# Ordering a two-block transformer's instructions with the compiler's other timing model

## The chip, the cores and the metric

The kernel runs on one NeuronCore of one Trainium2 chip. The metric is the device time of one execution in microseconds (us), lower is better. The core has five engines that run side by side, each through its own queue in order: PE (TensorE, matmul, with its weight loads shown as PEld), DVE (VectorE), ACT (ScalarE), POOL (GpSimd) and SP (SyncE, here only issuing DMAs). A queue in order means that an instruction which waits holds up all that stand behind it on that engine, even what could run.

## The reference, cut to what matters

The reference computes two blocks of two layers each on one sequence of 512 tokens of width 1024, in float32. Only what the text below speaks of is kept here:

```
def first_block(x, ...):
    for i in range(2):
        h = rmsnorm(x, norm_mix[i])
        x = x + (pool_mixer(h) if i == 0 else attn_mixer(h))       # dilated window attention, 16 heads
        h = rmsnorm(x, norm_ffn[i])
        x = x + swiglu(h, w_gate[i], w_up[i], w_down[i])
    return rmsnorm(x, norm_final)

def second_block(x, mem, ...):
    for l in range(2):
        z = rms_norm(x, ln_mix_pre[l]) @ w_in[l]
        branches = (nsa_mixer(...), retention_mixer(...), rwkv7_mixer(...), short_conv_mixer(...))
        merged = sum_m sigmoid(z_gate[m]) * (branches[m] @ w_branch[l, m])
        x = x + rms_norm(merged @ w_mix_out[l], ln_mix_post[l])
        x = x + rms_norm(cross_attention(...), ln_xa_post[l])
        x = x + rms_norm(square(relu(h @ mlp_w1[l])) @ mlp_w2[l], ln_mlp_post[l])
    return x

def rwkv7_mixer(...):      # state update, token after token
    def step(state, inp):
        sa = einsum('bhvk,bhk->bhv', state, -kk_t)
        state = state * w_t + sa x (kk_t * a_t) + v_t x k_t
        return state, einsum('bhvk,bhk->bhv', state, r_t)
```

## The kernel before, in words

All activations lie transposed, 128 features by 512 tokens to a tile. There are two kinds of work for PE.

**Dense products.** Each weight chunk of 128 output features (`wraw`, 512 KB) comes by a DMA from SP's queue, ACT copies it to a rounded half `whi` (line 346), DVE takes the rest `wlo` (line 347), and PE makes 24 matmuls of 128x512 from it: for each of eight depth slices hi*hi (line 356), hi*lo (357) and lo*hi (358). There are some 11,000 of these, and they need nothing but their weights and a free PSUM bank (tags `pmm` and `pr`).

**Chains.** Attention, the token recurrences and the norms go from PE to DVE or ACT and back, many times.
- The attention of the first block (`attention`) has 64 steps. One step is a score matmul (line 705), a DVE pass that adds the mask and takes the maximum (707), an ACT exponential (709), transposes on PE (721), an ACT copy (723) and value matmuls (729). Its PSUM tiles come from a ring of three banks (`pax`), one of which holds the output `po` meanwhile. While it runs, the products for the memory keys of layer 0 (`mem_kv`, 256 columns wide, operand `memhl`) can be made on PE; DVE empties them at line 889 and PE transposes them at line 895. `bias_tables` (lines 823, 834) can run there too.
- The sparse attention of the second block (`nsa`) has 32 steps of the same kind, eight for each block of 128 queries, over 128, 256, 384 and 512 keys: score 1403, DVE pass 1405, exponential 1407, transposes 1417, values 1425. Ahead of each block stands a small softmax (lines 1369 to 1388), and behind it a sum (1433 to 1438).
- `rwkv` is run twice a layer (j = 0 and 1), for two heads each. From the normed keys (1097) a row of full-width DVE instructions (1099 to 1119) prepares the operands, with a product on PE (1121) and transposes (1128, 1132). Then 1143 makes Gram matrices, and DVE solves a triangular system: lines 1146 to 1166 fill `sm`, POOL writes it to DRAM (1168) and reads it back spread over the partitions in eight DMAs (1172), and 14 rounds of three small instructions (1178 to 1180) run over it; 1198 and 1204 are the first matmuls that need the result. At last a chain of eight chunks runs over the tokens: 1252 (PE), 1254 (DVE), 1258 (PE), 1259 (DVE), 1265 (PE), 1267 (DVE), each needing the one before it, with 1275 and 1277 beside. `head_norm` (1013 to 1025) and the transposes 1281 end it. `retention` has a `head_norm` too, with transposes 1507.

The kernel gives no order of its own here. It is traced as one program; the compiler's scheduler then fills the queues of the engines. It keeps a simulated clock, and gives each engine what is ready by that clock, earlier in the program first; PSUM banks and buffers are handed out in the same run. So a dense product, which stands later in the program, is put into the stretch in which a chain's next step is not ready yet. How many of them are put there depends on how long the scheduler believes that a step takes.

## Time and profile before

| | us |
|---|---|
| median of three runs | 3450.81 |
| lowest and highest | 3436.98, 3454.37 |
| the profiled execution | 3444.46 |
| its span, from first to last instruction | 3442.7 |
| PE busy in it | 3344.2 (97%) |
| DVE, ACT, POOL busy | 1827.7, 1168.6, 399.7 |
| mean granted TensorE clock | 0.984 of 2.4 GHz |

By time the span holds the first block's pool mixer and feed-forward (to 587 us), attention (to 774), feed-forward (to 1236), the mixers of layer 0 (to about 1604, with the rest of their merge to 1847), cross attention and MLP (to 2365), and the same three of layer 1 (2365 to 3443). A view by windows gives the busy time of each engine in a stretch; the timeline gives single instructions in order; the granted clock is 1.00 at 2.4 GHz and 0.50 at 1.2 GHz.

### The profile page before, as it was taken

How to read it: one execution, taken by the hardware profiler on the slowest of the kernel's cores; microseconds unless marked ns; L12 is line 12 of the kernel's file. 1: busy time of each engine (PE TensorE's matmuls, PEld its weight loads, DVE VectorE, ACT ScalarE, POOL GpSimd, SP SyncE). 2: the span in 40 equal slices, each digit the busy share in tenths (PEclk: the TensorE clock that was granted, in tenths of full speed). 3: DMA queues.
4: the chain of work that ended last, by engine and by line, in shares of the span. 5: the costliest groups of instructions: out<-in, count | busy, mean ns of one | idle time of the engine just before them, and what ended most of it. 6: DMA issues, size and time to landing. Idle time of an engine off the chain costs nothing.

```text
span 3442.7 us, 41955 instructions
## 1 busy us (share of the span) xinstructions
PE 3344.2 (97%) x16382; PEld 2680.8 (78%) x16382; DVE 1827.7 (53%) x3340; ACT 1168.6 (34%) x1947; POOL 399.7 (12%) x332
## 2 busy tenths in 40 slices
PE   8999999999999999999999999998999999999997
PEld 6888888878888776777887788876777788688886
DVE  7554444445544565655455644566565644664445
ACT  4332232553222323322343433342332234343332
POOL 3200022001000210101220200022010121120001
PEclk9999999999999999999999999999999999999998
DMA  3323235242232230232242333333123223223332
GB/s 127 105 96 98 92 128 156 82 134 99 98 96 94 92 112 26 75 111 87 93 141 69 106 98 98 96 110 118 32 61 98 87 91 124 81 68 98 98 98 68
DMA packets 106262, 330.48 MB, mean 96 GB/s; under 512 B 13576, under 2 KB 17168, under 8 KB 103760
## 3 DMA queue, kind: packets, MB, share of 16 engines
q1 hardware_dynamic: 99856, 295.68, 26.6%
q10 hardware_dynamic: 3520, 23.48, 1.9%
q0 software_dynamic: 2688, 8.66, 1.1%
q8 instruction: 128, 2.10, 0.3%
q14 instruction: 70, 0.57, 0.1%
HBM read 307.56 MB, written 13.90 MB: 93 GB/s over the span
## 4 chain that ended last, share of the span: by engine, by line
PE 66%; DVE 7%; issue 2%; ACT 1%; POOL 0%; POOLq 0%; DVEq 0%; ACTq 0%
PE pmm L357 10%; PE pmm L358 10%; PE pmm L356 10%; PE pr L357 8%; PE pr L358 7%; PE pr L356 7%; PE pax L1403 1%; DVE hlo L395 1%; DVE pt L947 1%; PE pax L1425 1%; DVE x L950 1%; PE pr L1642 1%; DVE wlo L347 1%; PE pax L1544 1%; PE pax L1609 1%
## 5 line engine op out<-in xcount | busy, mean ns | idle before, releaser
L346 ACT ACTIVATE whi<-wraw 128x1024 fp32r<-128x1024 f32 (+3 forms) x593 | 565.0, 954 | 1606.1 <-PE pmm L357 627.0
L347 DVE TENSOR_TENSOR wlo<-wraw,whi 128x1024 fp32r<-128x1024 f32 (+3 forms) x593 | 653.1, 1102 | 217.9 <-ACT whi L346 213.1
L357 PE MATMUL pmm<-hlo,whi 128*128 128x512 f32 (+1 forms) x1504 | 598.9, 398 | 13.4 <-DVE hlo L395 13.2
L358 PE MATMUL pmm<-hhi,wlo 128*128 128x512 f32 (+1 forms) x1504 | 596.4, 397 | 1.7 <-DVE wlo L347 1.7
L356 PE MATMUL pmm<-hhi,whi 128*128 128x512 f32 (+1 forms) x1504 | 597.1, 397 | 0.0
L357 PE MATMUL pr<-hlo,whi 128*128 128x512 f32 (+1 forms) x1048 | 411.2, 392 | 10.4 <-DVE hlo L395 10.2
L356 PE MATMUL pr<-hhi,whi 128*128 128x512 f32 (+1 forms) x1048 | 410.6, 392 | 9.0 <-ACT whi L272 6.0
L358 PE MATMUL pr<-hhi,wlo 128*128 128x512 f32 (+1 forms) x1048 | 408.6, 390 | 0.9 <-DVE wlo L347 0.8
L431 POOL TENSOR_TENSOR sq<-sq 128x512 f32<-128x512 f32 (+1 forms) x130 | 182.1, 1401 | 1479.2 <-ACT sq L422 1371.7
L357 PEld LDWEIGHTS pmm<-hlo,whi 128*128 128x128 f32 x1504 | 285.4, 190 | 84.7 <-DVE hlo L395 19.9
L358 PEld LDWEIGHTS pmm<-hhi,wlo 128*128 128x128 f32 x1504 | 285.6, 190 | 64.3 <-DVE wlo L347 5.0
L356 PEld LDWEIGHTS pmm<-hhi,whi 128*128 128x128 f32 x1504 | 285.5, 190 | 58.7 <-issue 1.0
L357 PEld LDWEIGHTS pr<-hlo,whi 128*128 128x128 f32 x1048 | 199.7, 191 | 55.6 <-DVE hlo L395 15.4
L356 PEld LDWEIGHTS pr<-hhi,whi 128*128 128x128 f32 x1048 | 199.6, 190 | 51.3 <-ACT whi L272 6.0
L358 PEld LDWEIGHTS pr<-hhi,wlo 128*128 128x128 f32 x1048 | 199.1, 190 | 44.0 <-DVE wlo L347 4.0
L1551 POOL TENSOR_TENSOR macc<-macc,g 128x512 f32<-128x512 f32 x48 | 69.5, 1451 | 348.4 <-DVE g L1550 240.3
L356 PE MATMUL pr<-ahi,whi 128*128 128x512 f32 x240 | 93.4, 389 | 0.0
L357 PE MATMUL pr<-alo,whi 128*128 128x512 f32 x240 | 93.4, 389 | 0.0
L358 PE MATMUL pr<-ahi,wlo 128*128 128x512 f32 x240 | 93.4, 389 | 0.0
L356 PE MATMUL pmm<-ahi,whi 128*128 128x512 f32 x240 | 93.4, 389 | 0.0
L357 PE MATMUL pmm<-alo,whi 128*128 128x512 f32 x240 | 93.4, 389 | 0.0
L358 PE MATMUL pmm<-ahi,wlo 128*128 128x512 f32 x240 | 93.4, 389 | 0.0
(519 smaller groups left out, 5412.0 us busy)
## 6 DMA issues: line engine op xcount, KB each, us to landing
wraw<-w_in SPq DMA_DIRECT2D x116, 512.0 KB, 3.3
wraw<-mlp SPq DMA_DIRECT2D x64, 512.0 KB, 3.3
wraw<-mlp SPq DMA_DIRECT2D x128, 256.0 KB, 2.8
wraw<-ffn_g SPq DMA_DIRECT2D x44, 512.0 KB, 3.3
wraw<-ffn_u SPq DMA_DIRECT2D x44, 512.0 KB, 3.3
wraw<-wkv SPq DMA_DIRECT2D x32, 512.0 KB, 3.3
wraw<-ffn_d SPq DMA_DIRECT2D x32, 448.0 KB, 3.3
wraw<-qkv SPq DMA_DIRECT2D x24, 512.0 KB, 3.9
```

What stands on the lines that cost most here:

```text
L346: nc.scalar.activation(hi[:, :kt, :m], raw[:, :kt, :m], AF.Copy)
L347: nc.vector.tensor_sub(lo[:, :kt, :m], raw[:, :kt, :m], hi[:, :kt, :m])
L356: nc.tensor.matmul(ps[:, cols], hi[:, i], xh[:, k, cols], start=a, stop=False)
L357: nc.tensor.matmul(ps[:, cols], hi[:, i], xl[:, k, cols], start=False, stop=False)
L358: nc.tensor.matmul(ps[:, cols], lo[:, i], xh[:, k, cols], start=False, stop=z)
L395: nc.vector.scalar_tensor_tensor(lo, src, scale, hi, op0=OP.mult, op1=OP.subtract)
L431: nc.gpsimd.tensor_add(sq[:, c], acc[h][:, c], sq[:, c])
L947: nc.vector.scalar_tensor_tensor(t, y[:, n, cols], self.v(gname, n), r[:, cols], op0=OP.mult, op1=OP.mult)
L950: eng.tensor_add(x, x, t)
L1403: nc.tensor.matmul(ps[:, :nk], q[o, h // 2, qb * P:(qb + 1) * P], key[o, :nk], start=True, stop=True)
L1425: nc.tensor.matmul(poA[:, oc], eT[:, b * P:(b + 1) * P], vn[:, b * P + 64 * br:b * P + 64 * br + 64], start=b == 0, stop=b == qb)
L1551: nc.gpsimd.tensor_add(acc[:, n], acc[:, n], g)
```

## The change

One argument is given to the context in which the kernel is traced. The scheduler then orders the instructions with its other, finer timing of the machine. No instruction is added or taken away but for waits: the 14,900 matmuls are the same, and the sequences of POOL and SP are nearly so.

```
-    with tile.TileContext(nc) as tc:
+    with tile.TileContext(nc, schedule_with_timeline_sim=True) as tc:
         body(tc, a, vat)
```

**PE, late in the first block's attention.** `pmm` is a PSUM tile of a dense product for the memory keys, `pax` one of attention's. Before:

```order
L729 MATMUL pax<-vN,eT 128x64
L705 MATMUL pax<-kT,qz_3432 128x128
L721 MATMUL pax<-cst,e 128x128
L358 MATMUL pmm<-memhl,wlo 128x256
L356 MATMUL pmm<-memhl,whi 128x256
L357 MATMUL pmm<-memhl,whi 128x256
L705 MATMUL pax<-kT,qz_3432 128x128
L358 MATMUL pmm<-memhl,wlo 128x256
L895 MATMUL pr<-cst,vm 128x128 x2
L356 MATMUL pmm<-memhl,whi 128x256
L357 MATMUL pmm<-memhl,whi 128x256
L729 MATMUL pax<-vN,eT 128x64
```

The same place in the changed order:

```order
L705 MATMUL pax<-kT,qz_3432 128x128
L729 MATMUL pax<-vN,eT 128x64
L721 MATMUL pax<-cst,e 128x128
L729 MATMUL pax<-vN,eT 128x64
L705 MATMUL pax<-kT,qz_3432 128x128
```

The dense products have moved: the changed order puts 20 to 24 of them behind each of the fifth to the seventeenth score matmul, and the last 46 of the 64 have none behind them. Before, three or more stand behind nearly every one, to the end.

**DVE, in the triangular solve of layer 0, j = 1.** `sm` is what POOL sends to DRAM, line 1178 the first instruction that needs it back, 1405 the DVE pass of a step of the sparse attention. Before:

```order
L1166 SCALAR_TENSOR_TENSOR sm<-ac,pcst,sm 128x128
L1175 MEMSET y_9521 128x8
L1176 COPY y_9521<-sm 128x8
L1548 SCALAR_TENSOR_TENSOR macc<-g,pax 128x512 x2
L1539 TENSOR_TENSOR g<-pmm,rstd 128x512
L347 TENSOR_TENSOR wlo<-wraw,whi 128x1024
L1548 SCALAR_TENSOR_TENSOR macc<-g,pax 128x512
L1539 TENSOR_TENSOR g<-pmm,rstd 128x512
```

The changed order:

```order
L1166 SCALAR_TENSOR_TENSOR sm<-ac,pcst,sm 128x128
L1405 ISA e,nst<-pax,bd 128x512
L1405 ISA nst 128x1
L1176 COPY y_9521<-sm 128x8
L1405 ISA e,nst<-pax,bd 128x512
L1405 ISA nst 128x1
L1405 ISA e,nst<-pax,bd 128x512
L1405 ISA nst 128x1
L1178 TENSOR_TENSOR stmp<-y_9521,rwB 128x8
L1179 TENSOR_REDUCE y_9521<-stmp 128x8
L1405 ISA e,nst<-pax,bd 128x512
```

Between line 1176 and line 1178 stood 16 instructions of dense work before (of the merge of the branches); now the last block of queries of the sparse attention has moved here: three of its DVE passes stand ahead of line 1178, and four more behind it, between the rounds of the solve.

**PE, at the end of the recurrence of layer 0, j = 1.** Line 1252 begins a chunk of the token chain. Before:

```order
L1252 MATMUL pr<-S,rwA 64x128
L358 MATMUL pmm<-hhi,wlo 128x512
L356 MATMUL pmm<-hhi,whi 128x512
L357 MATMUL pmm<-hlo,whi 128x512
L1258 MATMUL pr<-R,rwB 64x64 x2
L358 MATMUL pmm<-hhi,wlo 128x512
L356 MATMUL pmm<-hhi,whi 128x512
L357 MATMUL pmm<-hlo,whi 128x512
L1265 MATMUL pr<-rwA 64x64
```

The changed order, at the last chunk:

```order
L1265 MATMUL pr<-rwA 64x64
L1252 MATMUL pr<-S,rwA 64x128
L1258 MATMUL pr<-R,rwB 64x64 x2
L1275 MATMUL pr<-rwA,rwB 64x64
L1277 MATMUL pr<-S,rwA 64x64
L1275 MATMUL pr<-rwA,rwB 64x64
L1277 MATMUL pr<-S,rwA 64x64
L1281 MATMUL pr<-cst,hc 128x128 x4
L1286 MATMUL pr<-rz,lora 128x512
L1507 MATMUL pax<-cst,hc 128x128 x4
```

The first chunks have 9 to 26 dense products ahead of most of their steps now, and the last three have none. The transposes 1281 follow the last chunk at once, where 64 dense products stood between them before. The same three moves are found in layer 1.

Over the whole PE queue, stretches of dense products between other matmuls were 370 before and are 219 now: 88 and 37 in attention, 109 and 62 in the mixers of layer 0, 109 and 58 in those of layer 1, the rest elsewhere.

## Rows read from the trace of the kernel before

**Rows 1.** The page, part 1: busy time, share of the span, instructions.

```profile
PE 3344.2 (97%) x16382; PEld 2680.8 (78%) x16382; DVE 1827.7 (53%) x3340; ACT 1168.6 (34%) x1947; POOL 399.7 (12%) x332
```

**Rows 2.** Windows: length, busy PE, PEld, DVE, ACT, POOL (instructions), clock, DMA, GB/s.

```profile
258.00:344.00 86.00, 86.00 (x381) 71.19 (x381) 36.86 (x44) 21.62 (x24) 0.00 (x0) 1.00 0.31 98
...
1236.00:1604.00 368.00, 360.25 (x2148) 261.39 (x2149) 217.37 (x572) 109.07 (x215) 28.88 (x34) 0.99 0.25 73
```

**Rows 3.** Timeline of PE: start, duration, line; three dense products between chain steps.

```profile
1527.03 0.50 PE L357 MATMUL pmm<-hlo,whi 128*128 128x512 f32 x1
...
1527.92 0.43 PE L1252 MATMUL pr<-S,rwA 128*64 128x128 f32 x2
```

**Rows 4.** Timeline of PE: one dense product between two chain steps.

```profile
1365.71 0.50 PE L358 MATMUL pmm<-hhi,wlo 128*128 128x512 f32 x1
1366.05 0.78 PE L1425 MATMUL pax<-rz,eT 128*128 128x64 f32 x6
```

**Rows 5.** Timeline of PE: one step of the first block's attention.

```profile
739.60 0.83 PE L705 MATMUL pax<-kT,qz 128*128 128x128 f32 x2
...
740.47 0.37 PE L358 MATMUL pmm<-memhl,wlo 128*128 128x256 f32 x1
...
740.99 0.60 PE L705 MATMUL pax<-kT,qz 128*128 128x128 f32 x1
```

**Rows 6.** Timeline of DVE in that step: the last read of the score's PSUM bank.

```profile
740.85 0.08 DVE L707 DVE_READ_ACCUMULATOR2_ANT astat<- 128x1 f32 x1
```

**Rows 7.** Windows: a wait of PE and what follows; the end of attention.

```profile
60.00:65.00 5.00, 0.12 (x1) 0.12 (x1) 5.00 (x13) 1.10 (x2) 1.35 (x1) 0.58 0.00 0
65.00:70.00 5.00, 5.00 (x12) 3.93 (x13) 4.30 (x11) 2.19 (x6) 0.00 (x0) 0.50 0.26 62
745.00:750.00 5.00, 4.13 (x15) 1.83 (x15) 1.85 (x10) 2.56 (x10) 0.00 (x0) 0.69 0.54 195
750.00:755.00 5.00, 4.71 (x23) 2.95 (x21) 2.13 (x4) 0.58 (x2) 0.00 (x0) 0.62 0.06 13
```

**Rows 8.** Timeline of DVE: ahead of the solve's way through DRAM; a sparse attention pass.

```profile
1431.85 1.29 DVE L1146 TENSOR_TENSOR rwB<-pr,pcst 128x512 f32<-128x512 f32 x2 [1.93 <-PE pr L1143]
...
1437.30 0.34 DVE L1166 SCALAR_TENSOR_TENSOR sm<-ac,pcst,sm 128x128 f32<-128x128 f32 x1
...
1413.18 0.69 DVE L1405 CUSTOM_DVE_ANT_0 e<-pax,bd 128x512 f32<-128x512 f32 x1 [1.49 <-PE pax L1403]
```

**Rows 9.** Timeline of POOL: the eight reads back from DRAM; below, their landing (line 1172).

```profile
1440.12 3.84 POOL L1172 DMA_DIRECT2D rwB<-a16d x8 [1.57 <-DMA a16d<-sm]
...
DMA to landing us min/median/max: 3.2/6.5/9.1
```

**Rows 10.** Timeline of PE: two transposes of the sparse attention, one step at 512 keys apart.

```profile
1408.85 0.61 PE L1417 MATMUL pax<-cst,e 128*128 128x128 f32 x4
...
1411.38 0.60 PE L1417 MATMUL pax<-cst,e 128*128 128x128 f32 x4
```

**Rows 11.** Timeline of DVE: first, small and last instructions of one head norm.

```profile
1536.14 0.69 DVE L1013 TENSOR_REDUCE hn<-pr 128x8 f32<-128x512 f32 x1 [1.70 <-PE pr L1277]
...
1550.59 0.17 DVE L408 SCALAR_TENSOR_TENSOR hn<-rs,hn 128x8 f32<-128x8 f32 x1
1550.79 0.17 DVE L406 TENSOR_TENSOR rs<-hn 128x8 f32<-128x8 f32 x1
...
1551.39 0.69 DVE L1025 TENSOR_TENSOR hc<-hc,hn 128x512 f32<-128x512 f32 x1
```

**Rows 12.** Timeline of DVE: the row of operands from 1099 to 1119, its ends.

```profile
1413.80 0.74 DVE L1099 SCALAR_TENSOR_TENSOR kkn<-rz,vec,pr 128x512 f32<-128x512 f32 x1
...
1419.68 0.74 DVE L1119 SCALAR_TENSOR_TENSOR sb<-rz,vec,kt 128x512 f32<-128x512 f32 x1
```

**Rows 13.** Timelines of PE and of DVE: one round trip of the chunk chain.

```profile
1529.18 0.44 PE L1258 MATMUL pr<-R,rwB 64*64 64x64 f32 x4
...
1529.66 0.29 DVE L1259 COPY rwA<-pr 64x128 f32<-64x128 f32 x1 [0.97 <-PE pr L1258]
```

## Prediction

> **What bounds the kernel now.** I read the page's busy times first, then windows of single stages, then the timelines of the stages that the order changes. The page says that PE is busy for 97% of the span [rows 1]: 3344.2 of 3442.7 us, so 98.5 us in which it does nothing. In a stretch of dense work it is busy all of the time and starts 381 matmuls in 86 us, 0.226 us each [rows 2]; DVE and ACT are busy for less than half of it. PE's own work is therefore the bound, and the same 14,900 matmuls stand in both orders. Only three things can change: what PE loses by waiting, what it loses in going from one kind of matmul to the other, and its clock. The mixers of a layer are the place with most to lose. There the chains run, and before the change PE is still busy for 360.25 of 368 us [rows 2]: each wait of a chain is covered by dense products.
>
> **The change, part by part.** *Fewer turns between kinds.* Three dense products between two steps of a chain take 0.89 us from the first start to the next chain matmul [rows 3]; at 0.226 each they are 0.68. So a stretch of dense products costs 0.21 us more than its matmuls. A stretch of one takes 0.34, which is 0.11 more [rows 4]. The order has 370 such stretches before and 219 after. I take the first price, since stretches of three and four are the commonest kind: 151 x 0.21 = 32 us gained, with 151 x 0.11 = 17 as the other end. Here a page of the Trainium skill speaks against the change: Perfetto Trace Analysis, section Optimization Strategy, advises to interleave stretches that are bound by different engines, and the new order takes them apart. The page puts no price on interleaving; this trace does, the 0.21 us. By the page alone this term would be no gain, and the time forecast below 32 us higher, 3562.
>
> *Attention of the first block.* The memory-key products are used up by the 17th of 64 steps. The other 46 run bare. One step before the change goes from score to score in 1.39 us, and its own matmuls have been started after 0.87 of it; the last 0.52 hold dense products [rows 5]. Without them the step gets no shorter: the next score starts at 740.99, right after the last read of a score's PSUM bank ended at 740.93 [rows 6], and that read hangs on the score before it. So 46 x 0.52 = 24 us become idle. The six of these steps that are 256 keys wide have more work of their own; at no idle time for them it is 21. No row excludes that ACT and DVE, with no memory keys to serve, shorten the step by up to a third, so 12 is the low end.
> When before the change the fill runs out, in the last steps, the clock falls: a mean of 0.69 and 0.62 of full speed in 745 to 755, with PE shown busy for 4.13 and 4.71 of each 5 us [rows 7]. At half clock a step's own work is 2 x 0.87 = 1.74 us, 0.35 above the 1.39. I take half of the 46 steps so: 8 us; the ends are 0 and 16. Attention: +32.
>
> *The mixers, once for each layer.* The new order spends 20 dense products (4.5 us) on each early step of the sparse attention, where 1 to 4 stood. Those steps now wait for nothing, but later steps find none left. I take the bare places in turn.
> (a) The solve, j = 1. DVE is busy from 1431.85 to 1437.64 with making `sm` [rows 8]; PE has about 1.4 bare attention steps to do meanwhile, and a step at 512 keys takes 2.53 us [rows 10], so it waits for 5.8 - 3.5 = 2.3. Then the way through DRAM: the last of the eight reads is issued by 1443.96 and lands 6.5 us after its issue at the median, 9.1 at most [rows 9], so 12.3 to 14.9 us after `sm`; I take 14, since the eight share the same engines and the last one is late. DVE stands at line 1178 all that time, with three of its attention passes done and four queued behind. PE's three steps last 3 x 2.53 = 7.6, so it waits for 6.4. The rounds behind are 42 small instructions at 0.20 [rows 11] and four passes of 0.69 [rows 8], 11.2 us and somewhat more, for 10.1 us of PE's steps: I take 2. Together 11 us. Before, some 230 dense products (52 us) lay over all this.
> (b) The last head norm of `rwkv`. It has four full-width passes of 0.69, one on ACT that I take as long, and 14 small ones 0.20 apart [rows 11]: 6.3 us alone. The new order pairs it on DVE, instruction by instruction, with retention's: 8 x 0.69 + 0.69 + 28 x 0.20 = 11.8 us, and the result that PE waits for is ready one pass before the end. PE has nothing between 1277 and 1281: 11 us.
> (c) Between 1097 and 1121, DVE makes the operands: 6.6 us [rows 12]. PE has some 1 us of small matmuls: 5.6.
> (d) The last three chunks. A round trip is 0.77 us from a matmul's start to the end of the DVE instruction behind it, and 0.44 of it are PE's [rows 13]: 0.33 idle, eleven times: 3.6.
> (e) In the j = 0 chunks some ten round trips stand as bare: 3.3.
> (f) The j = 0 head norm, 6.3 us and three attention passes of 0.69, against about 4.7 us of attention at 384 keys (2.53 x 3/4 a step, two and a half steps): 3.6.
> Sum: 11 + 11 + 5.6 + 3.6 + 3.3 + 3.6 = 38 us. What it does to the clock: after the 6 us wait at 60 the clock is at 0.50 in the next window, and PE starts 12 matmuls where full speed gives 22 [rows 7]; that is 2.3 us lost behind a long wait. Three long waits a layer ((a), (b), (c)) give 7, and 2 of that I set against dips that are there now: 5. So 43 a layer, 86 for both. Low end: half of the waits and no clock, 19 a layer. High end: 14.9 in (a) for 14, six more waits of 2 us where I saw cover, and twice the clock's 5: 61 a layer.
>
> *What is left as it is.* The dense stages (feed-forward, MLP, cross attention) keep their order but for a few products; SP's and POOL's queues too. The norms between stages get 37 products as cover where 17 stood and waited for little: 0.
>
> **How the numbers follow.** -32 + 32 + 86 = +86 us on the profiled 3444.5: 3530. That execution lies 6 us under the median of the three runs, 3450.81, and within their spread, so nothing is added. All terms at their low ends: -32 + 12 + 38 = +18, 3462; at their high ends: -17 + 24 + 16 + 122 = +145, 3589.
>
> **The rivals.**
> *Faster by the turns.* If the waits that I see are taken up, the 32 us of turns are what remains: 3412. The mechanism is the same bare stretch: the DVE pass of a step would have to come at once, so that PE runs scores ahead and finds work. For it speaks that at 512 keys PE runs bare steps without a break even now [rows 10]. Against it: line 1178 on DVE, which no free bank gets around, and the two head norms with nothing behind them on PE. It decides where all waits and clock together fall under 32 us; they were reckoned at 118. Chance 5%.
> *The same.* The products are only moved, and PE is 97% busy: what is lost late is gained early. But what an early step can gain is what it loses now, and in the mixers of a layer that is at most 7.75 us [rows 2]. This needs waits of about 32 us: 3445. Chance 6%.
> *Half of it.* The way through DRAM gets shorter in a stretch that loads few weights, and the rows of DVE run ahead: the low ends of the mixers with attention as forecast, 3444 - 32 + 32 + 38 = 3482. Chance 15%.
> *The clock.* In every bare stretch PE drops to 1.2 GHz and stays: attention's steps cost 0.35 more in all 46, 8 us above the forecast, and the eight bare steps of the last query block, whose 2.53 us are all PE's, cost twice that in both layers, 2 x 20: 3530 + 8 + 40 = 3578. For it speaks the fall to 0.62 where fill ends [rows 7]; against it that PE's share in the 512-key steps is full. Chance 14%. The Trainium skill, TensorE: Matmul & The Clock Gate, section What's actually happening, has it that the slow clock is the default and that activity releases it. By that rule this rival would have bare stretches at 1.2 GHz, 3578; the two windows at the end of attention agree as far as they go, and neither is at 0.50 for all its length.
> That the change does nothing is excluded by the order itself.
>
> The forecast's own case, 3495 to 3570, has the rest, 60%. The range runs from 3462 to 3600, the clock's case with some 20 us of further waits: it leaves out the first two rivals and little above. About 0.5% is what a measurement of this kernel can tell from no change, 3434 to 3468 around the median. Faster 5%, same 7%, slower 88%.
>
> **What would show it.** In the profile after: the late attention with PE idle or slow between scores at 1.4 us or more a step; DVE waiting for the DMA `rwB` ahead of line 1178, once or twice a layer; PE waiting for `hc` of line 1025 ahead of 1281 for about 11 us; PE waiting for `sb` ahead of 1121; fewer and longer stretches of dense products, and 0.226 us a matmul in them as before. The prediction is wrong if PE is idle for less than 150 us in all, if the stages outside attention and mixers change by more than some 5 us each, or if the turn from one kind of matmul to the other costs nothing in longer stretches.

## The result, and the profile after

The changed kernel takes 3592.72 us (median of four runs, 3591.20 to 3596.22), the kernel before, measured with it, 3451.23: 1.0418 times as long, 95% interval 1.0397 to 1.0439. The profiled execution has a span of 3589.4 us where before had 3442.7, 147 more.

Part 1 of the page after answers [rows 1], and the row PEclk of part 2 shows in 40 slices where the granted clock was below full speed (9 is full, 5 is half):

```profile
PE 3425.9 (95%) x16382; PEld 2758.4 (77%) x16382; DVE 1840.1 (51%) x3340; ACT 1169.4 (33%) x1947; POOL 406.1 (11%) x332
...
PEclk9999999969999999598999999999967899999998
```

PE does the same work in both. (The page has 16,382 records for the 14,900 matmuls of the program: a float32 product such as a score stands as two, so the 64 steps of line 705 are 128 records.) It is busy for 81.7 us more, and idle for 163.5 instead of 98.5. So 65 us of the 147 are idle time, and the rest is matmuls that take longer. The clock's row says which: three groups of slices stand at 5 to 8 (the last slice is at 8 before the change too). Windows of the attention before, then of the attention and of the mixers of layer 0 after the change (columns as in [rows 2]; the mixers end later because the stage is longer):

```profile
587.00:774.00 187.00, 182.83 (x1055) 152.68 (x1054) 81.98 (x242) 91.50 (x259) 9.90 (x16) 0.95 0.35 114
```

```profile
584.00:792.00 208.00, 193.21 (x1050) 160.38 (x1049) 83.72 (x243) 92.98 (x259) 9.88 (x16) 0.79 0.30 102
...
1259.00:1704.00 445.00, 414.97 (x2213) 303.87 (x2212) 221.83 (x578) 114.75 (x219) 31.82 (x35) 0.86 0.22 64
```

In the mixers PE is idle for 30.0 us where it was for 7.75, and a mean clock of 0.86 over 445 us means about 125 us at half speed. The trace's clock records have 126 there and 10 before the change, over the whole span 447 and 112. By stage, each from its first product on PE (lines 689, 1066) to the last of attention (791) or the first of cross attention (1609):

| stage, us | before | after | more |
|---|---|---|---|
| attention of the first block | 186.9 | 207.9 | 21.0 |
| mixers of layer 0, with the rest of their merge | 610.6 | 668.4 | 57.8 |
| the same of layer 1 | 611.2 | 666.5 | 55.3 |
| all else | 2034.0 | 2046.6 | 12.6 |

The new order draws 15 to 20 us a layer of merge products into the mixers, which is why the stage and its merge are taken together.

Where PE waits after the change (what it waits for: us in all, times, longest), the first lines of the list:

```profile
PE pr L357 <- DVE hlo L395: 16.8, 6, 7.0
PE pr L1281 <- DVE hc L1025: 14.8, 2, 7.4
PE pmm L356 <- ACT hhi L394: 14.7, 4, 5.7
PE pax L467 <- DVE rstv L408: 12.6, 3, 8.3
...
PE pr L1121 <- DVE sb L1119: 9.9, 2, 4.9
```

Lines 1281 and 1121 are waits that the forecast named, (b) and (c). Lines 356, 357 and 467 belong to the norms between the stages, which it had put at nothing; of these, line 467 waited for 12.5 us before as well. A wait of PE for the result of the solve (lines 1198, 1204) is not in the list at all.

The slow clock sits mostly in the sparse attention. Two windows, and the timeline of one step of its last block of queries, after the change:

```profile
1425.00:1440.00 15.00, 13.85 (x60) 9.01 (x61) 4.64 (x16) 2.52 (x8) 0.72 (x1) 0.51 0.00 1
1440.00:1460.00 20.00, 20.00 (x59) 11.13 (x60) 8.83 (x30) 5.99 (x14) 1.26 (x1) 0.50 0.00 0
```

```profile
1503.01 2.07 PE L1403 MATMUL pax<-mixw 64*128 64x512 f32 x2
1505.01 1.97 PE L1425 MATMUL pax<-rz,eT 128*128 128x64 f32 x8
1506.77 1.06 PE L1417 MATMUL pax<-cst,e 128*128 128x128 f32 x4
1507.76 2.07 PE L1403 MATMUL pax<-mixw 64*128 64x512 f32 x2
```

From 1440 to 1460 PE is shown busy for all of the 20 us (the ends of matmuls are modelled in these records), and has 0.50 of its clock. The step takes 4.75 us, with no break between its matmuls, where the same step took 2.53 before [rows 10].

### The profile page after: what moved, and what is told of

Read it like the earlier page. It is cut to its first block, busy times and chain, and to the rows that moved or that the text cites. A ratio compares the mean times of both kernels' runs of the same rounds, so it can differ in the third digit from the quotient of the medians.

```text
span 3589.4 us, 41924 instructions
## 1 busy us (share of the span) xinstructions
PE 3425.9 (95%) x16382; PEld 2758.4 (77%) x16382; DVE 1840.1 (51%) x3340; ACT 1169.4 (33%) x1947; POOL 406.1 (11%) x332
## 4 chain that ended last, share of the span: by engine, by line
PE 92%; DVE 6%; ACT 1%; issue 1%; DMA 0%; POOL 0%; DVEq 0%; ACTq 0%; POOLq 0%
PE pmm L357 14%; PE pmm L358 14%; PE pmm L356 14%; PE pr L357 11%; PE pr L358 11%; PE pr L356 10%; PE pax L1403 2%; PE pax L1425 2%; PE pax L705 1%; DVE pt L947 1%; PE pax L1417 1%; PE pax L1544 1%; PE pax L1546 1%; PE pax L1545 1%; PE pax L1609 1%; PE pr L1642 1%
## 5 line engine op out<-in xcount | busy, mean ns | idle before, releaser
L395 DVE SCALAR_TENSOR_TENSOR hlo<-x,vec,hhi 128x512 fp32r<-128x512 f32 (+1 forms) x88 | 93.7, 1089 | 4.8 <-ACT hhi L394 4.7
```

Of the source, the lines that this page charges most:

```text
L395: nc.vector.scalar_tensor_tensor(lo, src, scale, hi, op0=OP.mult, op1=OP.subtract)
```

## Experiments: where the time went

The first four kernels put the order of before back in one place at a time. The program is traced twice: once with the first timing model, to read its order, and again with an edge between neighbours of that order, for the instructions that one stage traces. The edges fix the sequence of an engine and wait for nothing. The kernel before, run beside these experiments, had medians of 3443 to 3445 us, and 3451 beside the result. So a difference of two medians can be off by some 7 us; "by the ratios" sets each run against the kernel before that ran beside it.

```
+ENGINES = ("PE", "DVE", "Activation")
...
+        for stage, s, e in spans:
+            if order and stage in stages:
+                last = {}
+                for n in order:
...
+                    if s <= n < e and engine in ENGINES:
+                        if engine in last:
+                            tc.add_manual_dep(traced[n], last[engine], NOSYNC, reason="pin")
+                        last[engine] = traced[n].name
...
+    order = trace(arrays, vat, False)[1]
+    nc = trace(arrays, vat, True, order, ('attention',))[0]
```

**e1_att_old: attention in the order of before.** The edit is the one above.

> The changed kernel, but in the first block's attention PE, DVE and ACT keep the order of before; all else in the new order. This undoes one place and shows what it is worth, whatever the cause. The stage from 584 to 792 us is 21 us longer after the change (207.9 against 186.9), so both theories expect 3593 - 21 = 3572 (3566 to 3578). If the stage's loss only moves on to the next stage, 3593.

Measured: 3572.92 us, 1.0378 of before (1.0356 to 1.0400). 20 us come back by the medians, 14 by the ratios. In its profile the stage has 186.2 us again. The place is worth about what its stage had grown.

**e2_mix_pe: PE alone, in the mixers.** `ENGINES = ("PE",)` and the stages `('mixers0', 'mixers1')`.

> The changed kernel, but in the mixers of both layers PE alone keeps the order of before; DVE, ACT, POOL and SP are ordered by the new timing model around it. Theory 1, the clock: what costs is that PE has stretches without dense products and falls to 1.2 GHz in them; then PE's order is all that matters and the 57.8 + 55.3 us by which the two layers' mixers with their merges grew come back: 3480 (3470 to 3490). Theory 2, the waits of the forecast's sum: part of the loss is in DVE's own order (the solve behind the attention passes, the two head norms in one), some 20 us a layer, which does not come back: 3520 or more.

Measured: 3509.02, 1.0185 (1.0158 to 1.0211), 84 us back (80 by the ratios). It lies between the theories: PE's order is most of it, not all.

**e2_mix_old: PE, DVE and ACT, in the mixers.** As above with the three engines.

> As e2_mix_pe (the changed kernel with the mixers of both layers in the order of before), but DVE and ACT keep the order of before there too, not PE alone. With PE alone the time fell from 3593 to 3509. If PE's order is all that counts: 3509 again (within 6). If DVE's and ACT's own order holds the remaining 30 us of the two layers' 113: 3480 (3474 to 3488).

Measured: 3477.80, 1.0113 (1.0078 to 1.0148), 115 us back (105 by the ratios), where the two layers had grown by 113. So 25 to 31 us lie in the order of DVE and ACT. With PE alone held, the two layers of the table together last 30 us longer than with all three held. PE is idle in them for 9.7 us more, and has 41 us more at half clock, half of which is 20. DVE, ordered for the other model, seems to serve the same PE order a little late, with the clock behind it; which of its instructions are late was not followed.

**e12_old: both places.**

> The changed kernel with both the first block's attention and the mixers of both layers in the order of before (PE, DVE, ACT); the new order is left in the dense stages: pool mixer, feed-forward, cross attention, MLP and the norms between them. The forecast put these at nothing, their stage lengths after the change say some +10 in all: 3443 to 3460. If it is over 3465, the places between the stages cost more than was taken.

Measured: 3458.81, 1.0045 (1.0026 to 1.0064). The parts add up (3592.72 - 20 - 115 = 3458), and 15 us (9 to 22 by the interval) are left in the dense stages, at the upper end of what was expected. In its profile PE is busy for 3344.1 us as before, and idle for 113.8 instead of 98.5: here it is waits. The waits of PE in the kernel before, and then in this one, for the lines of the norms:

```profile
PE pmm L357 <- DVE hlo L395: 13.2, 13, 1.6
...
PE pr L357 <- DVE hlo L395: 10.2, 9, 3.5
...
PE pr L356 <- ACT hhi L394: 3.0, 2, 2.2
```

```profile
PE pr L357 <- DVE hlo L395: 17.8, 6, 7.0
...
PE pmm L356 <- ACT hhi L394: 14.7, 4, 5.7
PE pmm L357 <- DVE hlo L395: 10.8, 4, 5.3
PE pr L356 <- ACT hhi L394: 6.6, 2, 4.4
```

Before, the norms had many waits of 1 to 2 us; now there are fewer, the longest of 4 to 7. At the norm near 1800 us PE had 30 products of cover ahead of line 467 and 50 behind it, and then waited 1.72 and 0.95 us. In this kernel 57 stand ahead of line 467 and four behind it, and PE waits 5.72 and 2.41. That the order of these products is the cause is read from the trace; no run put it back by itself.

## Experiments: is it the clock or the waits?

**c_bare: fill taken out where the steps are PE's own work.** The kernel before; PE's queue of the mixers gets one edit, and the edges above hold it.

```
+            at = [queue.index(n) for n in marks[int(stage[-1])]]
+            a0, a1 = min(at), max(at) + 1
+            block = queue[a0:a1]
+            queue[a0:a1] = [n for n in block if n not in dense] + [n for n in block if n in dense]
```

`marks` are the scores and value products of the last block of queries, `dense` what lines 356 to 358 make.

> The kernel before, with one edit of PE's queue: in the mixers of each layer the 59 dense products that stand between the first score and the last value product of the last block of queries (512 keys) are moved behind that stretch. Its eight steps, with the preparation of j = 1 beside them, are bare, as in the changed order; everything before and after keeps the order of before. Of the 49 us that the stretch took, 59 x 0.23 and some ten turns of 0.21 go elsewhere: some 33 us of PE's own work stay. Theory 1, the clock: PE falls to 1.2 GHz in the bare stretch though it has work all the time, and loses up to 33 us a layer, 25 as a guess: 3443 + 50 = 3493 (3475 to 3510). Theory 2, waits: at 512 keys a step is bound by PE's own matmuls, 2.53 us; the row of operands on DVE gives at most 5 us of waits, ten turns fewer take 2 back: 3443 to 3449.

Measured: 3493.25, 1.0139 (1.0116 to 1.0161): 49 us slower, as the clock's theory has it. The stretch in windows, and one step:

```profile
1383.00:1400.00 17.00, 14.05 (x31) 6.43 (x31) 7.09 (x23) 2.64 (x6) 1.99 (x2) 0.50 0.00 0
1400.00:1420.00 20.00, 20.00 (x61) 12.43 (x60) 10.29 (x34) 7.88 (x16) 0.00 (x0) 0.50 0.00 0
```

```profile
1408.74 2.07 PE L1403 MATMUL pax<-mixw 64*128 64x512 f32 x2
1410.75 1.97 PE L1425 MATMUL pax<-rz,eT 128*128 128x64 f32 x8
1412.51 1.06 PE L1417 MATMUL pax<-cst,e 128*128 128x128 f32 x4
1413.50 2.07 PE L1403 MATMUL pax<-mixw 64*128 64x512 f32 x2
```

The clock falls at 1380.9, behind a wait of 0.79 us for line 1417, and stays at 0.50 for 51 us. From 1400 to 1420 PE has no idle time in the records, and the step takes 4.76 us for 2.53. The mixers of the two layers are 25 and 23 us longer, of which 6 each are idle; the rest is the clock (55 us of each at 0.50, for 10 and 14). The same products, moved by 50 us, cost 1.4% of the kernel.

**c_fill: the same stretch with useless products.** One line more than c_bare, ahead of each score of the last block:

```
+                for i in range(7 if order and qb == 3 else 0):
+                    nc.tensor.matmul(out, self.pnhi[:, i, :P], self.pnhi[:, i], start=True, stop=True)
```

> c_bare (the 59 dense products moved behind the last block of queries, 3493) with work added that leads to nothing: ahead of each of the block's eight scores PE makes seven dummy products 128x512 into the score's own PSUM bank, 56 a layer where 59 real ones stood. They are 56 x 0.226 + 8 x 0.21 = 14 us of PE's time a layer. Theory 1, the clock: the stretch keeps 2.4 GHz, the 25 us a layer that c_bare lost come back, and 14 are paid: 3493 - 2 x 11 = 3471 (3462 to 3480), faster with more work. Theory 2, the order itself: c_bare lost by what was moved, not by the clock; the dummies only add: 3493 to 3521.

Measured: 3483.67, 1.0108 (1.0092 to 1.0124), 9.6 us less than c_bare, with 112 products more. The two sets of four runs just touch (3487.82 is the lowest there, 3487.94 the highest here). The same windows as above, and one step:

```profile
1383.00:1400.00 17.00, 12.59 (x47) 7.75 (x47) 8.10 (x25) 3.83 (x9) 1.99 (x2) 0.80 0.00 0
1400.00:1420.00 20.00, 20.00 (x97) 12.52 (x95) 11.42 (x35) 7.76 (x16) 0.00 (x0) 1.00 0.00 1
```

```profile
1410.05 1.12 PE L1403 MATMUL pax<-mixw 64*128 64x512 f32 x2
1411.11 1.10 PE L1425 MATMUL pax<-rz,eT 128*128 128x64 f32 x8
1412.05 0.60 PE L1417 MATMUL pax<-cst,e 128*128 128x128 f32 x4
1412.41 1.88 PE L1744 MATMUL pax<-hhi 128*128 128x512 f32 x7
1414.22 1.12 PE L1403 MATMUL pax<-mixw 64*128 64x512 f32 x2
```

Here too the clock falls behind the wait for line 1417, at 1385.7, but it is back after 6.8 us, and then it is 1.00 in the window in which it was 0.50. Nothing but work on PE was added. So the clock falls at the short wait in both, and the bare steps do not bring it back. A step takes 4.17 us: 2.53 of its own and 1.64 of filler, still less than 4.76 at half clock. The time is 13 us above the expectation, for the greater part since PE is idle for 12.6 and 12.9 us in the mixers of the two layers, 5 more than before; c_bare has that too. The Trainium skill, TensorE: Matmul & The Clock Gate, section What's actually happening, has it that the array's default is the slow clock and that activity releases it. These two runs agree with that: work alone brings 0.50 back to 1.00. A full busy share in the profile was not enough for it: c_bare has it at 0.50.

**d_mix and d_mix7: useless products in the changed kernel.** The order of the changed kernel, with three or seven dummies ahead of each of the last 16 scores of the sparse attention:

```
+            self.spare(ps[:, :nk], self.pnhi, 7, qb > 1); nc.tensor.matmul(ps[:, :nk], q[o, h // 2, qb * P:(qb + 1) * P], key[o, :nk], start=True, stop=True)
```

> The changed kernel with the same order of PE, and 96 products more: ahead of each score of the last two blocks of queries of the sparse attention, in both layers, PE makes three dummy products 128x384 or 128x512 into the score's own PSUM bank, which the score then overwrites. At 0.17 and 0.226 us they are 9.5 us a layer, with 16 turns at 0.21 some 13. Theory 1, the clock: of the 125 to 132 us a layer at 1.2 GHz the 92 between the last chunks of j = 0 and the solve go back to full speed; that gives some 45 us a layer, and about 10 of them go to waits that come to light (the solve's way through DRAM, the operands' row on DVE): 3593 - 2 x 22 = 3550 (3530 to 3570). Theory 2, waits: the dummies add their work or hide in waits: 3593 to 3619. What of the forecast's waits was real can be read here at full clock: PE's wait at the solve, forecast at 8.4 us a layer, and ahead of line 1121, 5.6.

> As d_mix (the changed kernel with dummy products ahead of the sparse attention's last 16 scores), but seven for each score instead of three, which did not hold the clock (0.50 to 0.56 in the windows from 1425 to 1480 us). 112 a layer, some 25 us at full clock with their turns. Theory 1, the clock: seven hold it, some 45 us a layer come back, 25 are paid, and waits of some 8 us come to light, the solve's way through DRAM among them: 3593 - 2 x 12 = 3569 (3550 to 3590). If seven don't hold it either, they cost twice their time: 3593 + 100 = 3690.

Measured: 3612.81 with three, 1.0487 (1.0464 to 1.0510), and 3603.82 with seven, 1.0460 (1.0445 to 1.0475): 20 and 11 us slower than without (24 and 14 by the ratios). The windows, of three and then of seven dummies:

```profile
1440.00:1460.00 20.00, 20.00 (x59) 11.32 (x58) 8.28 (x29) 5.17 (x14) 1.01 (x1) 0.50 0.00 0
1460.00:1480.00 20.00, 19.79 (x65) 13.67 (x65) 8.15 (x31) 6.50 (x14) 0.25 (x1) 0.50 0.00 1
```

```profile
1441.00:1465.00 24.00, 20.77 (x108) 13.75 (x108) 11.89 (x37) 8.46 (x20) 1.27 (x1) 0.99 0.00 0
...
1510.00:1537.00 27.00, 25.35 (x156) 17.09 (x155) 14.66 (x61) 8.77 (x20) 0.00 (x0) 1.00 0.13 38
```

Three did not hold the clock, and cost their time mostly at half speed. So d_mix says nothing against the clock; it only shows that not every filler does it. Seven held it in these windows. The mixers then have 85 and 72 us at half clock instead of 126 and 133: half of the 41 and 61 us that are gone is 20 and 30 us gained. 25 us a layer were paid for the dummies, and 5 us of idle time came to light, twice. The balance is +9 and 0 by this account, +10.3 and +3.4 by the stage lengths. The expectation had 45 us coming back, which was too much: the stretches that hold no score, ahead of 1121 and around 1281, stayed slow. The expected totals were missed in both runs (d_mix lies in the range of the waits, 3593 to 3619, d_mix7 above the clock's 3590). The windows of d_mix7 at 0.99 and 1.00 speak for the clock all the same.

**d_att: useless products in the changed attention.** Three dummies of 256 columns behind each of the last 47 scores.

```
+            nc.tensor.matmul(ps[:, :nk], self.cls(qh(h), g, b), key, start=True, stop=True); self.spare(ps[:, 256:], kT.bitcast(F32R), 3, it in late)
```

> The changed kernel with the same order of PE, and 141 products more: behind each of the last 47 scores of the first block's attention PE makes three dummy products 128x256 (kT in the dense products' number format), whose result nobody reads. By a third of a 512-wide dense product's 0.226 us to a half of it they are 11 to 16 us of work that leads to nothing. Theory 1, the clock: the 85 us at 1.2 GHz between 702 and 787 us go back to 2.4 GHz, a step from 1.54 to the 1.39 us that it took before, and the tail behind the steps shortens: about 16 us less, 3577 (3570 to 3585), with the mean granted clock up by 0.012. Theory 2, waits: PE's idle time in these steps is taken up by the dummies, the chain from score to score is as long as it was: 3593, or up to 16 us more, 3609.

Measured: 3610.51, 1.0490 (1.0464 to 1.0515), 18 us slower. This is against the clock's expectation, but the dummies held the clock for a part only: it is 1.00 to 727 us, and the stage still has 72 us at 0.50 where the changed kernel has 85. The steps, first of the changed kernel (half clock), then with the dummies at full clock, then with them at half clock:

```profile
731.40 0.83 PE L705 MATMUL pax<-kT,qz 128*128 128x128 f32 x2 [0.29 <-DVE astat L707]
...
732.95 0.83 PE L705 MATMUL pax<-kT,qz 128*128 128x128 f32 x2 [0.18 <-DVE astat L707]
```

```profile
712.07 0.83 PE L705 MATMUL pax<-kT,qz 128*128 128x128 f32 x2 [0.28 <-DVE astat L707]
...
713.82 0.83 PE L705 MATMUL pax<-kT,qz 128*128 128x128 f32 x2 [0.28 <-DVE astat L707]
```

```profile
730.74 0.83 PE L705 MATMUL pax<-kT,qz 128*128 128x128 f32 x2 [0.18 <-DVE astat L707]
...
732.92 0.84 PE L705 MATMUL pax<-kT,qz 128*128 128x128 f32 x2 [0.18 <-DVE astat L707]
```

The bare step takes 1.55 us at half clock, 0.16 more than the 1.39 of before at full clock [rows 5]. With dummies it takes 1.75 at full clock and 2.18 at half. PE waits for the DVE pass of line 707 in all three: the step is a loop from score to score, and what is put into it makes it longer. So if a bare step at full clock took the 1.39 of before, the clock is worth 46 x 0.16 = 7 us here, and the loop has the rest, as the forecast had it. A bare step of this form at full clock was not seen in any run; the nearest, in the changed kernel from 697.70 to 699.10 us, has a transpose and two value products more and took 1.40. The dummies stood in the score's own PSUM bank, so whether they held up the DVE pass itself stays open.

**warm: the same idea in the kernel before.** Order kept; dummies ahead of nine instructions that wait.

```
+        ps = self.pax(); self.spare(ps[:, P:], "stat_sum")
...
+        pb = self.pax(); self.spare(pb, "stat_end")
```

> The kernel before, order kept, with 50 dummy products (weights of 64 columns, 384 or 512 wide, one tile of constants as operand) put on PE right ahead of nine instructions for which it waits 1.05 to 2.5 us: the norms' sums of line 449 at 128, 493 and 821 us, the transposes of line 467 at 1187 and 2337, and lines 1317 and 1313 of both layers. They fill the waits to about 0.7 to 0.9 of their length and delay nothing. Theory 1, the clock: behind these waits the clock falls to 0.50 for 3.4 us at a time (10 behind 1182), seven times, each worth half of that; with the waits filled it does not fall: 3444 - 12 = 3432 (3426 to 3438). Theory 2: a wait that short takes nothing with it, the falls have another cause: 3444, or up to 5 more where a dummy is late.

Measured: 3441.42 against 3444.70, ratio 0.9991 (0.9980 to 1.0002): no difference that this measurement can tell. Two of the windows, of before and of this kernel, and one window of the mixers of this kernel:

```profile
120.00:134.00 14.00, 12.95 (x54) 10.14 (x53) 4.33 (x5) 5.13 (x11) 6.51 (x7) 0.88 0.41 141
488.00:502.00 14.00, 12.95 (x54) 10.04 (x53) 4.56 (x16) 2.20 (x3) 2.21 (x2) 0.88 0.69 257
```

```profile
120.00:134.00 14.00, 13.61 (x64) 10.81 (x63) 2.58 (x3) 4.94 (x11) 6.53 (x8) 1.00 0.39 124
488.00:502.00 14.00, 13.73 (x64) 11.51 (x65) 2.69 (x14) 1.49 (x2) 0.22 (x1) 1.00 0.33 115
...
1322.00:1342.00 20.00, 20.00 (x189) 14.37 (x186) 7.64 (x27) 5.70 (x12) 0.72 (x1) 0.74 0.08 28
```

The falls behind these waits of 1.05 us are gone. A wait of 1 us can take the clock along, but it need not: in c_bare, where nothing fills them, the same waits at 128.9 and 818.1 took nothing with them and the one at 492.1 did. So these windows do not show that the filler did it. And the 12 us are not there: the mixers of the two layers are 3.0 and 1.8 us longer, with a new fall at 1331 where PE has work throughout. Why it fell there is open; before has 1.00 in the same place. No kernel here beats the one before by more than the measurement can tell.

## Why the prediction was right, and where it was not

The forecast was 3530 us with a range of 3462 to 3600. The time of 3592.72 is inside and the direction is right, but 63 us above the forecast, nearest to the rival called the clock, 3578. It lies outside the forecast's own case, 3495 to 3570. The range held because it had been drawn up to the clock's case with 20 us of waits on top. The forecast's own sum of waits did not bring the time inside it, so the hit is in part luck. Of the three signs of being wrong none came: PE is idle for 163.5 us, the stages outside changed by at most some 5 us each (12.6 in all), and the turns have their price. By its own terms:

- **Turns, -32: the price held; no run took the term by itself.** At full clock, a stretch of dense products costs about 0.2 us more than its matmuls at 0.226, whatever its length: 0.21 for those of three before (median of 54), 0.22 for those of 17 to 40 after (median of 65). The other end, 0.11 for stretches of one, was a single row; the median of 54 such stretches is 0.18. At that price 151 stretches fewer are the 32 us. If they were gained, the clock took more than three times as much over the whole span (147 more in all, less 65 idle, plus 32 gained: 114).
- **Attention, +32, or +21 net of its turns: the sum held, its split did not.** 21.0 by the stage, 14 to 20 by e1_att_old. PE waits for `astat` between bare scores, and the steps take 1.55 us. But of the 24 us that were to become idle only 10.6 did (14.8 in the stage against 4.2): all steps from 702 us on stand at half clock, not half of them, and the slow matmuls fill a part of the wait. The forecast's 8 us for the clock is near the 7 of the step lengths.
- **Mixers, 43 a layer: mis-sized, about 57 net of the turns where 33 were forecast.** Idle time grew by 22 us a layer in the mixers (30.0 against 7.75) and by some 2 in the rest of the merge, where 38 had been forecast. The turns give back 10, which leaves some 43 for the clock, where the forecast had put 5. Its waits were too large in three terms. (a) *The solve:* its first wait came, while DVE makes `sm`: 3.1 us ahead of line 1438, forecast 2.3. The way through DRAM is as long as forecast. `sm` is done at 1495.2, and line 1178 starts 13.5 us later (forecast: 14); DVE's timeline after the change:

```profile
1494.83 0.35 DVE L1166 SCALAR_TENSOR_TENSOR sm<-ac,pcst,sm 128x128 f32<-128x128 f32 x1
...
1508.72 0.17 DVE L1178 TENSOR_TENSOR stmp<-y,rwB 128x8 f32<-128x8 f32 x1 [2.80 <-issue]
```

But PE does not wait for it: at 4.75 us a step the three steps last 14 us, not 7.6. The slow clock hides the wait that was forecast at full clock. Where the clock is up, the wait comes to light: in layer 1 of d_mix the last three steps run at full clock, and PE then waits 3.5 us for the solve's result (line 1198). In d_mix7 the dummies make the steps long enough, and it does not. Bare steps at full clock, and with them the forecast's 6.4 us, are in no run. (b) *The two head norms:* 7.4 us, not 11. (c) *The operands' row:* 4.9 for 5.6. (d), (e): the round trips of the bare chunks leave PE 0.38 to 0.42 us each, for 0.33, 5.5 a layer for 6.9. (f): PE does not wait for the j = 0 head norm; at half clock the attention steps cover it.
- **Norms between the stages, 0: wrong, +15** by e12_old. The forecast counted the cover, and not whether it stands where PE waits.

The step that failed is the one against the clock's rival: "against it that PE's share in the 512-key steps is full". The forecast took the fall of the clock for something that comes behind a long wait, and gave each wait 2.3 us. A full busy share does not hold the clock, and does not bring it back: in c_bare it is 20.00 of 20 us and the clock 0.50. The evidence was in its own rows: in 745 to 755 [rows 7] the clock fell with PE shown busy for 4.13 and 4.71 of 5 us, right where the dense products ran out. The trace of before has more of it, in the sparse attention itself: the clock falls at 1398.9 us, for 6.8 us, with no wait of PE ahead of it (and so in layer 1, at 2528.7).

```profile
1392.00:1398.00 6.00, 6.00 (x27) 3.33 (x26) 4.47 (x10) 3.24 (x7) 1.92 (x1) 1.00 0.00 0
1398.00:1406.00 8.00, 8.00 (x17) 3.56 (x16) 4.75 (x12) 4.80 (x10) 0.25 (x1) 0.57 0.17 66
```

And the sum priced waits at full clock and the clock as an addition to them, though the two replace each other: a slow PE has work for longer and waits less. In the mixers 22 us more of waits stood against 38 forecast, and some 43 us for the clock against 5.

The forecast also set the Trainium skill, Perfetto Trace Analysis, section Optimization Strategy (interleave stretches that are bound by different engines), against the 32 us of the turns. These runs agree with the advice: taken apart, the stretches lose 105 to 115 us in the mixers by e2_mix_old, turns included.

## What to carry to other kernels

Dense products between the steps of a chain do more than fill idle time: they keep PE's clock up, also where the chain alone would keep PE busy without a break. So before products are moved out of a stretch, price the stretch at half clock (here 2.2 us for each attention step of 2.53), read the granted clock of every window beside the busy share, and do not add waits of full clock on top. Filler work pays only where it is cheaper than the half clock: real products have to be made anyway, seven dummies a step gave back 0.6 us of 4.76 in c_fill and lost 11 us in all in d_mix7, and inside a loop that PE waits for they cost more than they give.

## What the runs showed of the hardware that was not expected

- PE shown busy for 20.00 of 20 us can be at 0.50 of its clock for all of them (after, 1440 to 1460; c_bare, 1400 to 1420), and the clock can fall with no wait ahead (before, 1398.9).
- Small DVE instructions of two chains share their time. One chain has them 0.20 us apart [rows 11]; in the paired head norms two stand in 0.20 us, so that both norms take the 0.20 of one:

```profile
1652.53 0.24 DVE L406 TENSOR_TENSOR rs<-hn 128x8 f32<-128x8 f32 x2
...
1652.94 0.24 DVE L408 SCALAR_TENSOR_TENSOR hn<-rs,hn 128x8 f32<-128x8 f32 x2
...
1654.34 1.29 DVE L1025 TENSOR_TENSOR hc<-hc,hn 128x512 f32<-128x512 f32 x2
```

Each row is two instructions, one of each norm. The two norms together take 7.9 us, from 1647.77 to 1655.63, where the forecast had 11.8, and two by themselves would be 2 x 6.3 by its count; pairing independent chains on DVE, taken by itself, is a gain.
- The price of a turn between the two kinds of matmul, about 0.2 us, does not depend on the length of the stretch (medians of 0.13 to 0.29 for classes from one product to forty, and no trend).
